# MLP up projections as seven block products of eight, on sums of token halves that stay on chip

## The chip, the cores and the metric

One Trainium2 chip, and one of its cores. A core has five engines that each run their own list of instructions strictly in order: TensorE (PE) for matmuls, VectorE (DVE), ScalarE (ACT), GpSimd (POOL) and SyncE (SP); they wait for one another by semaphores, and DMA queues move data between HBM and the core's memory, SBUF. Matmul results land in eight banks of PSUM. The metric is the time of one execution on the device, in microseconds; the figure for a kernel is the median of several executions.

## The reference

A trunk of four layers on 512 tokens of width 1024. A layer has a token mixer (gated linear attention, latent attention, a gated convolution, gated linear attention again), then an MLP with 4096 hidden columns, then a gated per-layer embedding. The change touches the MLP alone:

```python
for i in range(DEPTH):                       # DEPTH = 4
    h = ...                                  # the mixer of layer i
    x = layer_norm(ALPHA * x + h, ln_g[i, 0], ln_b[i, 0])
    x = layer_norm(ALPHA * x + sq_relu_mlp(x, mlp_w1[i], mlp_w2[i]), ln_g[i, 1], ln_b[i, 1])
    ...                                      # the per-layer embedding

def sq_relu_mlp(x, w1, w2):                  # x 512x1024, w1 1024x4096, w2 4096x1024
    return jnp.square(jax.nn.relu(x @ w1)) @ w2
```

All of it is float32.

## The kernel before

**Three matmuls for one.** TensorE takes a reduced float32 (fp32r). To keep float32 accuracy each operand is split into a high part (a cast on ScalarE) and a low part (the operand less its high part, on VectorE); `split` (L86) does it in pieces of 128 x 1024, and `mm3` (L112) issues high by high, high by low and low by high (L114 to L116). Weights come from HBM by SyncE (`wget`, L90, four buffers of 1 MB named raw) and are split into four slots (`wsplit`, L95, tiles wh and wl). Token-side operands and hidden values are tiles r of a ring of ten buffers of 1 MB; t tiles are temporaries, xn the residual rows, ps the PSUM banks.

**The MLP** (L230). The hidden columns are taken in eight groups of 512. `up(g)` computes a group: four blocks of 128 columns, for each 8 steps of the inner dimension by three matmuls that hold 128 x 128 of the weights still and move 512 tokens (a record with `ps<-r,wh`, 128x512). Relu and square on ScalarE (L233, L234) leave the hidden tile. The first group runs in two halves of 256 tokens (128x256), because the transposes of the last tokens come in between (`ln_tr`, L160, which transposes normalised rows on TensorE and splits them). The operand x is split once, in four ring buffers.

`down(g)` (L258) takes two groups of hidden values, 512 tokens by 1024 hidden, against 1024 x 1024 of the second weights, as seven block products of eight (a block scheme of the Strassen kind). Blocks of a are formed in place on VectorE (L303, L305, L313, L315). Sums of weight blocks are made by accumulating DMAs, which GpSimd issues (`wadd`, L106): the buffer `chain` gets b22, then b12 is added, it is split for product 2, then b11 is added, split for product 3, then b21 is added, split for product 5; `both` is b12 plus b11, for product 6. Each product is 2 x 4 x 3 matmuls that move 512 weight columns (`ps<-wh,r`, 128x512). VectorE adds each result into xn (L286, L288); the last down of a layer also starts its layer norm.

**Order.** TensorE's order is the order in which the program is written: up 0, up 1, then (up 2, down 0, up 3), (up 4, down 1, up 5), (up 6, down 2, up 7), down 3. The lists of the other engines are ordered by a scheduler when the program is built. A tile from a pool waits until the instruction that last used its buffer is done, and a DMA into it waits likewise.

## Time and profile before

| | |
|---|---|
| median of three runs | 2403.24 us (2403.14 to 2404.35) |
| profiled execution's own time | 2404.62 us |
| its span | 2402.0 us |
| the four MLPs in it | 244 to 573, 808 to 1137, 1378 to 1707, 2006.5 to 2335.5 us |
| TensorE busy in the first of these | 328.86 of 329.00 us |
| HBM read, written | 323.64 MB, 8.39 MB |
| accumulating loads of 1 MB | 64 in the program, 16 a layer |
| plain loads of MLP weights of 1 MB | 144, 5.0 us to landing in the median |

The times come from the runs, the rest from one profiled execution, whose span runs from its first instruction to its last; the 2.6 us between span and own time lie around it. A view that lists instructions gives the start, the duration, the engine, the line in the program, the operation, out<-in by the program's names, and in brackets the idle time before it and what released it. A group's row gives the count, then busy time and mean duration in ns, then the engine's idle time before those instructions. Matmuls overlap: a record's duration is longer than the distance to the next one. For DMAs, "to landing" is the time from the issue until the data is there.

### The profile page before, as it was taken

The page shows a single profiled execution, that of the slowest core. Times are in us where ns is not written, and L with a number is a line of the kernel's source. Part 1 is how long each engine was busy: PE and PEld are TensorE (multiplying, and loading weights), DVE is VectorE, ACT ScalarE, POOL GpSimd, SP SyncE. Part 2 cuts the span into 40 slices and gives each one's busy share as a digit, 9 for nine tenths or more (in the row PEclk, how much of TensorE's full clock was granted, in tenths as well). Part 3 has the DMA queues.
Part 4 walks back from the last instruction along what each step waited for, and adds up shares of the span by engine and source line. Part 5 has one row for each costly group of instructions (what it writes and reads, how often), then busy time and mean ns, then how long its engine had stood idle before and what let it go on. Part 6 is the DMA issues. An engine that isn't in the chain of part 4 may idle for free. (4 is left out here: it accounts for less than half of the span.)

```text
span 2402.0 us, 28355 instructions
## 1 busy us (share of the span) xinstructions
PE 2374.6 (99%) x11394; PEld 1994.7 (83%) x11394; DVE 1549.8 (65%) x1964; ACT 1078.2 (45%) x1542; POOL 260.4 (11%) x264
## 2 busy tenths in 40 slices
PE   8999999999999999999999999999999999999998
PEld 7888888888888888888888888888887888888887
DVE  6777466469687654577744646656957766645775
ACT  6353445445464354444422244445444443544452
POOL 1541000000000100000000000000005511000000
PEclk9999999999999999999999999999999999999999
DMA  6222565674323356665424256567441224566650
GB/s 226 79 92 102 134 180 141 159 197 158 118 84 110 120 129 173 193 177 165 145 101 158 71 140 186 152 154 201 155 130 62 89 104 123 141 158 192 187 155 35
DMA packets 64563, 334.90 MB, mean 139 GB/s; under 512 B 6704, under 2 KB 19760, under 8 KB 28080
## 3 DMA queue, kind: packets, MB, share of 16 engines
q1 hardware_dynamic: 52272, 256.55, 30.6%
q0 software_dynamic: 9856, 68.16, 15.1%
q10 hardware_dynamic: 2304, 8.39, 1.0%
q8 instruction: 89, 1.46, 0.2%
q14 instruction: 42, 0.34, 0.0%
HBM read 323.64 MB, written 8.39 MB: 138 GB/s over the span
## 5 line engine op out<-in xcount | busy, mean ns | idle before, releaser
L88 DVE TENSOR_TENSOR wl<-raw,wh 128x1024 fp32r<-128x1024 f32 x510 | 623.5, 1238 | 452.2 <-ACT wh L87 448.6
L87 ACT CAST wh<-raw 128x1024 fp32r<-128x1024 f32 x510 | 520.3, 1049 | 585.0 <-PE ps L115 245.6
L114 PE MATMUL ps<-r,wh 128*128 128x512 f32 (+1 forms) x1896 | 714.9, 377 | 4.0 <-ACT r L87 4.0
L115 PE MATMUL ps<-r,wh 128*128 128x512 f32 (+1 forms) x1896 | 710.6, 375 | 1.5 <-DVE r L88 0.9
L116 PE MATMUL ps<-r,wl 128*128 128x512 f32 (+1 forms) x1896 | 710.0, 374 | 0.0
L114 PE MATMUL ps<-wh,r 128*128 128x512 f32 x1328 | 520.1, 392 | 0.0
L116 PE MATMUL ps<-wh,r 128*128 128x512 f32 x1328 | 517.0, 389 | 0.0
L115 PE MATMUL ps<-wl,r 128*128 128x512 f32 x1328 | 516.7, 389 | 0.0
L114 PEld LDWEIGHTS ps<-r,wh 128*128 128x128 f32 x1896 | 357.8, 189 | 67.3 <-ACT r L87 5.0
L115 PEld LDWEIGHTS ps<-r,wh 128*128 128x128 f32 x1896 | 357.7, 189 | 66.3 <-DVE r L88 4.2
L116 PEld LDWEIGHTS ps<-r,wl 128*128 128x128 f32 x1896 | 357.5, 189 | 63.9
L116 PEld LDWEIGHTS ps<-wh,r 128*128 128x128 f32 x1328 | 249.3, 188 | 52.2
L115 PEld LDWEIGHTS ps<-wl,r 128*128 128x128 f32 x1328 | 249.5, 188 | 50.6
L114 PEld LDWEIGHTS ps<-wh,r 128*128 128x128 f32 x1328 | 249.4, 188 | 50.5
L88 DVE TENSOR_TENSOR r<-r,r 128x1024 fp32r<-128x1024 f32 x112 | 136.4, 1221 | 80.9 <-ACT r L87 80.9
L87 ACT CAST r<-r 128x1024 fp32r<-128x1024 f32 x112 | 116.7, 1049 | 136.8 <-PE ps L116 80.2
L107 POOL DMA_DIRECT2D raw<-in_mlp_w x64 | 55.9, 874 | 1085.4 <-DVE wl L88 633.3
L288 DVE TENSOR_TENSOR xn<-xn,ps 128x512 f32<-128x512 f32 x192 | 130.6, 680 | 57.7 <-PE ps L116 57.7
L233 ACT ACTIVATE t<-ps 128x512 f32<-128x512 f32 x128 | 76.0, 594 | 143.6 <-PE ps L116 143.6
L146 POOL TENSOR_TENSOR rs<-rs,nhalf 128x1 f32<-128x1 f32 (+2 forms) x44 | 59.7, 1358 | 685.2 <-DVE rs L145 685.2
L87 ACT CAST r<-ps 128x512 fp32r<-128x512 f32 x84 | 46.5, 591 | 95.2 <-PE ps L164 80.9
L480 ACT ACTIVATE t<-t 128x512 f32<-128x512 f32 (+2 forms) x64 | 37.4, 590 | 107.0 <-POOL t L544 77.0
(192 smaller groups left out, 1864.0 us busy)
## 6 DMA issues: line engine op xcount, KB each, us to landing
raw<-in_mlp_w SPq DMA_DIRECT2D x144, 1024.0 KB, 5.0
raw<-in_mlp_w POOLq DMA_DIRECT2D x64, 1024.0 KB, 8.4
raw<-in_ple_gate SPq DMA_DIRECT2D x16, 1024.0 KB, 5.1
raw<-in_conv_in SPq DMA_DIRECT2D x12, 1024.0 KB, 5.1
raw<-in_gla_v SPq DMA_DIRECT2D x8, 1024.0 KB, 5.5
raw<-in_gla_r SPq DMA_DIRECT2D x8, 1024.0 KB, 4.9
raw<-in_gla_out SPq DMA_DIRECT2D x8, 1024.0 KB, 5.0
xd<-t SPq DMA_DIRECT2D x24, 256.0 KB, 3.9
```

The costliest lines, as they stand in the source:

```text
L87: A.copy(h, src)
L88: return V.tensor_tensor(out=l, in0=src, in1=f(h), op=ALU.subtract)
L107: G.dma_start(dst, ap, accum_op=ALU.add)
L114: PE.matmul(o, ah, bh, start=start, stop=False, skip_group_check=more)
L115: PE.matmul(o, ah, bl, start=False, stop=False, skip_group_check=more)
L116: PE.matmul(o, al, bh, start=False, stop=stop, skip_group_check=more)
L146: G.tensor_tensor(out=dst, in0=dst, in1=nhalf[:, :n], op=ALU.pow)
L233: A.activation(r, ps, AF.Relu)
L288: V.tensor_tensor(out=z, in0=z, in1=ps, op=op)
L480: exps.append(A.activation(o, a, AF.Exp, scale=1.0 / TAU))
```

## The change

**Up becomes seven products of eight.** A group of 512 hidden columns is seen as two halves of 256 columns, the inner dimension as two halves of 512, the tokens as two halves of 256. Seven products, named 1, 2, 7, 6, 4, 5, 3 in the order in which they run, take the place of eight: each multiplies a 512 x 256 block (or sum of blocks) of the weights with a 512 x 256 block (or sum) of the tokens, 2 x 4 x 3 = 24 matmuls that move 256 tokens. TensorE's list grows from 10,476 to 12,396 matmul and transpose rows.

**Token sums.** `add_norm` leaves the transposed tokens unsplit (`raw_tr`). `form(p)` makes the operand of product p in place from the quarters of x (a11, a21, a12, a22) and splits it; each is made once a layer and kept for all eight groups, in seven of now eleven ring buffers. The temporaries lose one buffer.

**Weight sums.** The host lays the first weights out in quarters. Per group: w0 (two loads of 0.5 MB, products 1 and 2), w2 (a load of 1 MB and an accumulating load of 1 MB, products 7 and 5), w3 (two VectorE adds in w0's buffer, products 6 and 4), w1 (0.5 MB, product 3).

**Results.** Products 1, 6 and 7 are copied out of PSUM by ScalarE; products 2, 4 and 5 are combined with these copies on VectorE; then relu and square as before, in the new lines L306 and L307.

**Order.** Two groups, then down, four times. The last product of a group is held and runs after products 1 and 2 of the next group, or after the first product of down; the last product of down runs after products 1 and 2 of the next group. The first two groups of a layer are interleaved (`first_groups`).

The diff, without blank lines and a few repeats:

```diff
@@ -53,9 +53,9 @@
-    r8 = ctx.enter_context(tc.tile_pool(name="r8", bufs=10))
+    r8 = ctx.enter_context(tc.tile_pool(name="r8", bufs=11))
...
-    t2 = ctx.enter_context(tc.tile_pool(name="t2", bufs=8))
+    t2 = ctx.enter_context(tc.tile_pool(name="t2", bufs=7))
...
@@ -165,6 +165,13 @@
             sl = slice(t * P, t * P + P)
             split(xh[c][:, :, sl], xl[c][:, :, sl], ps)
 
+    def raw_tr(t, z, xr):
+        for c in range(2):
+            ps = bank().rearrange("p (k q) -> p k q", q=P)
+            for k in range(4):
+                PE.transpose(ps[:, k, :], z[:, (c * 4 + k) * P : (c * 4 + k + 1) * P], ident)
+            A.copy(xr[c][:, :, t * P : t * P + P], ps)
+
     def new_xT():
         xh = [ring([P, 4, T], F32R) for _ in range(2)]
         xl = [ring([P, 4, T], F32R) for _ in range(2)]
@@ -211,8 +218,8 @@
             for t in range(NT):
                 hk = pre(t) if hf == 0 and pre else {}
                 if hf == 1 and t >= 2:
-                    new = new or [new_xT()]
-                    hk = {4: lambda t=t: ln_tr(t - 2, xn[t - 2], *new[0])}
+                    new = new or [[ring([P, 4, T]) for _ in range(2)]]
+                    hk = {4: lambda t=t: raw_tr(t - 2, xn[t - 2], new[0])}
                 ps = nat_group(lhs, ws, t, hk)
                 z = xn[t][:, hf * 512 : hf * 512 + 512]
                 if scaled:
@@ -235,28 +242,143 @@
         hid = {}
+        forms = {}
+        xq = [x[c][:, :, h * 256 : h * 256 + 256] for c in range(2) for h in range(2)]
+        def form(p):
+            if p not in forms:
+                a11, a21, a12, a22 = xq
+                if p == 7:
+                    V.tensor_tensor(out=a11, in0=a11, in1=a21, op=ALU.subtract)
+                elif p == 6:
+                    V.scalar_tensor_tensor(out=a11, in0=a11, scalar=-1.0, in1=a22, op0=ALU.mult, op1=ALU.subtract)
+                elif p == 5:
+                    V.tensor_tensor(out=a21, in0=a22, in1=a21, op=ALU.subtract)
+                elif p == 3:
+                    V.scalar_tensor_tensor(out=a11, in0=a11, scalar=-1.0, in1=a12, op0=ALU.mult, op1=ALU.subtract)
+                st = forms[p] = ring([P, 2, 4, 256], F32R)
+                split(st[:, 0], st[:, 1], {1: a11, 7: a11, 6: a11, 3: a11, 2: a12, 4: a22, 5: a21}[p])
+            return forms[p]
         def up(g):
-            ws = [v3(wload(I["mlp_w1"][i, 2 * g + u]), 256) for u in range(2)]
-            hid[g] = ring([P, 4, T])
-            if g > 0:
-                for fb in range(4):
-                    hidden_out(stat_group(ws[fb // 2], fb % 2, x), hid[g], fb)
-                return
...
+            raw = [None] * 4
+            w = {}
+            bk = {}
+            kept = {}
+            half = slice(0, 1024), slice(1024, 2048)
+            def weights(p):
+                src = I["mlp_w1"][i, g]
+                if p in (1, 2) and raw[0] is None:
+                    raw[0] = wraw.tile([P, 2048], F32, tag="raw", name=nm("raw"))
+                    for h, c in zip(half, (0, 3)):
+                        SP.dma_start(raw[0][:, h], src[:, c * 1024 : c * 1024 + 1024])
+                    w[0] = v3(wsplit(raw[0]), 256)
+                if p in (7, 5) and raw[2] is None:
+                    raw[2] = wget(src[:, 1024:3072])
+                    wadd(raw[2], src[:, 0:2048])
+                    w[2] = v3(wsplit(raw[2]), 256)
+                if p in (6, 4) and raw[3] is None:
+                    a, b = (raw[0][:, h] for h in half)
+                    V.tensor_tensor(out=a, in0=a, in1=raw[2][:, half[1]], op=ALU.add)
+                    V.tensor_tensor(out=b, in0=b, in1=a, op=ALU.add)
+                    raw[3] = raw[0]
+                    w[3] = v3(wsplit(raw[3]), 256)
+                if p == 3:
+                    raw[1] = wget(src[:, 2048:3072], 1024)
+                    w[1] = v3(wsplit(raw[1], 1024), 256)
+                n, k0 = {1: (0, 0), 2: (0, 4), 7: (2, 4), 5: (2, 0), 6: (3, 0), 4: (3, 4), 3: (1, 0)}[p]
+                return w[n], k0
+            def quarter(th, hf):
+                if g not in hid:
+                    hid[g] = ring([P, 4, T])
+                return hid[g][:, 2 * hf : 2 * hf + 2, th * 256 : th * 256 + 256]
...
+            def act(o, src, scale=1.0):
+                r = tmp()
+                A.activation(three(r), src, AF.Relu, scale=scale)
+                A.activation(o, three(r), AF.Square)
+            def product(p):
+                name = {1: "b", 2: "d", 7: "c", 6: "b", 4: "c", 5: "b", 3: "b"}[p]
+                (wh, wl), k0 = weights(p)
+                st = form(p)
+                first = name not in bk
+                if first:
+                    bk[name] = bank()
+                ps = bk[name]
+                for cb in range(2):
+                    o = ps[:, cb * 256 : cb * 256 + 256]
+                    c = slice(cb * P, cb * P + P)
+                    for k in range(4):
+                        mm3(o, (wh[:, k0 + k, c], wl[:, k0 + k, c]), (st[:, 0, k, :], st[:, 1, k, :]),
+                            first and k == 0 and cb == 0, k == 3, not first or cb == 1)
+                if p in (1, 6):
+                    t = kept[p] = tmp()
+                    A.copy(t, ps)
+                elif p == 7:
+                    t = kept[p] = tmp()
+                    A.mul(t, ps, -1.0)
+                elif p == 2:
+                    z = quarter(0, 0)
+                    V.tensor_tensor(out=z, in0=three(kept.pop(1)), in1=three(ps), op=ALU.add)
+                    act(z, z)
+                elif p == 4:
+                    z = quarter(1, 0)
+                    V.tensor_tensor(out=z, in0=three(kept.pop(6)), in1=three(ps), op=ALU.add)
+                    act(z, z)
+                elif p == 5:
+                    z = quarter(1, 1)
+                    V.tensor_tensor(out=z, in0=three(kept.pop(7)), in1=three(ps), op=ALU.subtract)
+                    act(z, z)
+                else:
+                    act(quarter(0, 1), three(ps), -1.0)
+            return product
+        held = []
+        def release():
+            while held:
+                held.pop(0)()
+        def group(g):
+            u = up(g)
+            u(1)
+            u(2)
+            release()
+            for p in (7, 6, 4, 5):
+                u(p)
+            held.append(lambda: u(3))
+        def first_groups():
+            u, n = up(0), up(1)
+            u(1)
+            raw_tr(2, xn[2], x)
+            u(2)
+            n(1)
+            raw_tr(3, xn[3], x)
+            n(2)
+            for p in (7, 6, 4, 5):
+                u(p)
+            n(7)
+            u(3)
+            for p in (6, 4, 5):
+                n(p)
+            held.append(lambda: n(3))
         def down(g, gb=None):
-            h0, h1 = hid.pop(2 * g), hid.pop(2 * g + 1)
+            h0, h1 = hid[2 * g], hid[2 * g + 1]
             lo, hi = slice(0, 256), slice(256, 512)
             a11, a21, a12, a22 = h0[:, :, lo], h0[:, :, hi], h1[:, :, lo], h1[:, :, hi]
             sts = [small(12, f"st{t}", 1) for t in range(NT)] if gb is not None else None
@@ -267,10 +389,13 @@
                 return I["mlp_w2"][i, hf, 2 * g + c]
-            def product(a, w, name, th, hf, op):
+            def ready(a, w):
                 st = ring([P, 2, 4, 256], F32R)
                 split(st[:, 0], st[:, 1], a)
-                wh, wl = v3(wsplit(w), 512)
+                return st, v3(wsplit(w), 512)
+            def product(st, w, name, th, hf, op):
+                wh, wl = w
                 for q in range(2):
                     first = (name, q) not in banks
                     if first:
@@ -299,29 +424,32 @@
             b11, b12, b21, b22 = weights(0, 0), weights(1, 0), weights(0, 1), weights(1, 1)
             chain = wget(b22)
             wadd(chain, b12)
-            product(a11, wget(b11), "b", 0, 0, add)
+            product(*ready(a11, wget(b11)), "b", 0, 0, add)
+            release()
             V.tensor_tensor(out=a11, in0=a11, in1=a21, op=sub)
-            product(a11, chain, "c", 1, 1, sub)
+            product(*ready(a11, chain), "c", 1, 1, sub)
             V.scalar_tensor_tensor(out=a11, in0=a11, scalar=-1.0, in1=a22, op0=ALU.mult, op1=sub)
             wadd(chain, b11)
-            product(a11, chain, "b", 1, 0, add)
+            product(*ready(a11, chain), "b", 1, 0, add)
             wadd(chain, b21)
-            product(a12, wget(b21), "d", 0, 0, add)
+            product(*ready(a12, wget(b21)), "d", 0, 0, add)
             both = wget(b12)
             wadd(both, b11)
-            product(a22, chain, "c", 1, 0, add)
+            product(*ready(a22, chain), "c", 1, 0, add)
             V.tensor_tensor(out=a21, in0=a22, in1=a21, op=sub)
-            product(a21, both, "b", 1, 1, sub)
+            product(*ready(a21, both), "b", 1, 1, sub)
             V.scalar_tensor_tensor(out=a11, in0=a11, scalar=-1.0, in1=a12, op0=ALU.mult, op1=sub)
-            product(a11, wget(b22), "b", 0, 1, sub)
-        up(0)
-        up(1)
-        for g in range(3):
-            up(2 * g + 2)
-            down(g)
-            up(2 * g + 3)
-        down(3, load_gb(i, 1))
+            parts = ready(a11, wget(b22))
+            held.append(lambda: product(*parts, "b", 0, 1, sub))
+            if gb is not None:
+                release()
+        first_groups()
+        for g in range(4):
+            if g:
+                group(2 * g)
+                group(2 * g + 1)
+            down(g, load_gb(i, 1) if g == 3 else None)
         return new_xT()
     def ple(i, x, xn, last):
...
+def _quad(w):
+    u = _stat(w).reshape(-1, 2, P, 2, 1024)
+    return np.concatenate([u[:, c, :, r] for r, c in ((0, 0), (0, 1), (1, 1), (1, 0))], axis=-1)
...
-    o["mlp_w1"] = np.stack([_stat(w) for w in a["mlp_w1"]])
+    o["mlp_w1"] = np.stack([_quad(w) for w in a["mlp_w1"]])
...
-    nc = bacc.Bacc("TRN2", target_bir_lowering=False, num_devices=1, dynamic_dma_scratch_size=4096)
+    nc = bacc.Bacc("TRN2", target_bir_lowering=False, num_devices=1, dynamic_dma_scratch_size=2048)
```

**How the order moves: down's fifth product.** ScalarE's list in the second down of a layer, before; raw_459 is the buffer `chain`, wh_472 its split for product 3 and wh_482 that for product 5, r_481 the operand of product 5, raw_480 the buffer `both`.

```order
L87 CAST wh_472_3125<-raw_459_3040 128x1024 [waits DMASW6_49]
L234 ACTIVATE r_450_2927<-t_454_2981 128x512 [waits Activation_49]
L87 CAST wh_472_3125<-raw_459_3040 128x1024
...
L87 CAST r_475_3160<-r_435_2798 128x1024 [waits PE_49]
L87 CAST wh_482_3203<-raw_459_3040 128x1024 [waits DMASW7_49]
L87 CAST wh_482_3203<-raw_459_3040 128x1024
L87 CAST r_481_3200<-r_435_2798 128x1024 [waits PE_49]
L87 CAST wh_485_3239<-raw_480_3197 128x1024 [waits DMASW5_49]
```

The same list in the change; raw_473 is `chain`, wh_485 its split for product 2, wh_490 for product 3, wh_500 for product 5; r_499 is the operand of product 5, raw_498 is `both` and wh_503 its split for product 6.

```order
L87 CAST wh_485_3260<-raw_473_3181 128x1024 [waits DMASW0_49,PE_49]
...
L87 CAST wh_490_3299<-raw_473_3181 128x1024 [waits DMASW2_49]
...
L87 CAST wh_500_3377<-raw_473_3181 128x1024 [waits DMASW3_49]
L87 CAST wh_500_3377<-raw_473_3181 128x1024
L87 CAST wh_503_3413<-raw_498_3371 128x1024 [waits DMASW1_49]
L87 CAST wh_503_3413<-raw_498_3371 128x1024
L87 CAST r_499_3374<-r_457_3017 128x1024 [waits DVE_49,PE_49]
```

The operand of product 5 now stands behind the split of the sixth product's weights, not ahead of it. The wait for PE at wh_485 is for the slot that product 4 of the second group used last; the semaphore DMASW is that of the accumulating load.

**How the order moves: the first groups.** ScalarE's list in the change, from the last transposes on (r_334 and r_335 are the raw tokens, r_371 the operand of product 7, r_376 that of product 6; wh_388 is the split of a 0.5 MB weight for product 3, in a slot that products 1 and 2 of the second group used last):

```order
L173 COPY r_335_1903<-ps_364_2122 128x4x128 [waits PE_49]
L87 CAST wh_388_2337<-raw_387_2335 128x1024 [waits DMAHW0_49,PE_49]
L87 CAST r_371_2168<-r_334_1902 128x1024 [waits DVE_49]
L306 ACTIVATE t_367_2155<-r_366_2153 128x512 [waits DVE_49]
L307 ACTIVATE r_366_2153<-t_367_2155 128x2x256 [waits Activation_49]
L87 CAST r_376_2207<-r_334_1902 128x1024 [waits DVE_49]
```

And VectorE's at the same place:

```order
L255 TENSOR_TENSOR r_334_1902<-r_334_1902 128x4x256 [waits Activation_49]
...
L88 TENSOR_TENSOR wl_389_2338<-raw_387_2335,wh_388_2337 128x1024 [waits DMAHW0_49,Activation_49]
L88 TENSOR_TENSOR r_371_2168<-r_334_1902,r_371_2168 128x1024 [waits Activation_49]
L257 SCALAR_TENSOR_TENSOR r_334_1902<-r_334_1902,r_335_1903 128x4x256 [waits DVE_49]
L88 TENSOR_TENSOR r_376_2207<-r_334_1902,r_376_2207 128x1024 [waits Activation_49]
```

Before, the tokens' splits stood here, straight out of the transposes; now a weight's cast and its subtraction come ahead of the operand of product 7, and three operations in place stand between the transposes and the operands.

11 lines of the change are left out of this document (2 added, 9 removed).

## The prediction

> **What bounds the kernel now.** I read the busy times first, then the slices, then the groups, then stretches.
>
> ```profile
> span 2402.0 us, 28355 instructions
> PE 2374.6 (99%) x11394; PEld 1994.7 (83%) x11394; DVE 1549.8 (65%) x1964; ACT 1078.2 (45%) x1542; POOL 260.4 (11%) x264
> PE   8999999999999999999999999999999999999998
> DVE  6777466469687654577744646656957766645775
> DMA  6222565674323356665424256567441224566650
> ```
>
> TensorE is busy 99% of the span and no other engine comes near. The stretch of the first MLP (from 244 to 573 us; the other three are alike) shows the same:
>
> ```profile
> core 0: us, PE busy (x) PEld busy (x) DVE busy (x) ACT busy (x) POOL busy (x), PEclk, DMA share, GB/s
> 244.00:573.00 329.00, 328.86 (x1550) 276.42 (x1549) 200.59 (x207) 152.06 (x183) 17.04 (x18) 1.00 0.61 168
> ```
>
> TensorE pauses 0.14 us in 329. So each matmul taken away is paid in full, and each new wait of TensorE costs in full. VectorE, at 200.59 of 329 (61%), and the DMA engines, at 0.61, have room, but not endless room.
>
> **The gain: matmuls times spacing.** A matmul record's duration overlaps the next one, so I take the spacing from starts that lie far apart in unbroken runs:
>
> ```profile
> 394.28 0.39 PE L114 MATMUL ps<-wh,r 128*128 128x512 f32 x1
> ...
> 424.20 0.39 PE L114 MATMUL ps<-wh,r 128*128 128x512 f32 x1
> 245.45 0.28 PE L114 MATMUL ps<-r,wh 128*128 128x256 f32 x1
> ...
> 247.61 0.28 PE L114 MATMUL ps<-r,wh 128*128 128x256 f32 x1
> ```
>
> The 512-wide pair is 132 matmuls apart: 29.92 / 132 = 0.2267 us. The 256-wide pair is 18 apart: 2.16 / 18 = 0.120 us. Two halves therefore cost 0.240, 6% more than one whole.
>
> Per layer, up has been seven groups of 4 x 8 x 3 = 96 wide matmuls (672) and the first group in halves (192 narrow): 672 x 0.2267 + 192 x 0.120 = 175.4 us. It becomes 8 groups x 7 products x 24 = 1344 narrow ones: 161.3 us. The gain is 14.1 us a layer, 56.4 in all; of the 23.1 that seven wide products would save (672 x 0.2267 = 152.3), 9.0 go to the narrow form. Down keeps its 7 x 24 wide matmuls per call, 5.44 us a product.
>
> [...]
>
> **What is added beside TensorE.** The rows that price it:
>
> ```profile
> L88 DVE TENSOR_TENSOR wl<-raw,wh 128x1024 fp32r<-128x1024 f32 x510 | 623.5, 1238 | 452.2 <-ACT wh L87 448.6
> L87 ACT CAST wh<-raw 128x1024 fp32r<-128x1024 f32 x510 | 520.3, 1049 | 585.0 <-PE ps L115 245.6
> L88 DVE TENSOR_TENSOR r<-r,r 128x1024 fp32r<-128x1024 f32 x112 | 136.4, 1221 | 80.9 <-ACT r L87 80.9
> L305 DVE SCALAR_TENSOR_TENSOR r<-r,r 128x1024 f32<-128x1024 f32 x16 | 19.6, 1223 | 0.4
> L233 ACT ACTIVATE t<-ps 128x512 f32<-128x512 f32 x128 | 76.0, 594 | 143.6 <-PE ps L116 143.6
> L288 DVE TENSOR_TENSOR xn<-xn,ps 128x512 f32<-128x512 f32 x192 | 130.6, 680 | 57.7 <-PE ps L116 57.7
> ```
>
> A group has seven split pieces on VectorE instead of four, two adds of raw weights and three additions out of PSUM; 3 x 1.24 + 2 x 1.22 + 3 x 0.68 = 8.2 us a group, 65 a layer, and 13 more for the seven token sums with their splits, less the eight splits of 512 columns that the old transposes had. VectorE goes to about 275 of 330, 83%. ScalarE gets 24 more casts, 24 PSUM copies and seven casts of sums: 24 x 1.05 + 24 x 0.59 + 7 x 1.05 = 47 more, 60%. A group loads 3.5 MB instead of 2 (0.5 + 0.5, 1 plus an accumulated 1, 0.5), 12 MB more a layer on the 168 GB/s x 329 us = 55 MB there now: the DMA share goes from 0.61 to about 0.75. All three stay under TensorE, so averages cost nothing; I walked the steady cycle (two groups and a down, 14 x 2.88 + 7 x 5.44 = 78.4 us of TensorE) engine by engine, and looked for places where something comes late in order. The PSUM copies, the smaller ring of temporaries, the eleventh ring buffer and the smaller scratch I cost at nothing: their consumers lie several products behind. If that cover is gone, a late PSUM copy is one row of 0.59 us per product, at most 56 x 0.59 = 33 us a layer if all were bare, which I leave out of the range, since ScalarE has 40% of its time free.
>
> **First wait: the first groups.** The tokens' transposes now come raw, and the sums are made after them. Product 1 waits for the VectorE split of its sum behind the layer norm's tail, about 0.8 us beyond its place. Product 7 needs the sum a11 - a21. On ScalarE its cast stands behind a weight cast (wh_388) whose slot is freed only when the second group's product 2 ends, and that is the last work ahead of product 7. VectorE's order has that weight's split ahead of the sum's as well. So from there 1.05 (weight cast) + 1.24 (its split, with the sum's cast beside it) + 1.22 (the sum's split) = 3.5 us. Product 6 needs an update (1.22), a cast (0.95 back to back) and a split (1.22), 3.6 with hand-overs against product 7's 24 x 0.120 = 2.9: 0.7. Together 5.0, less the 0.3 that the start of an MLP waits today (two starts 0.42 apart below, where 0.12 is the spacing), 4.7 a layer. Bounds for product 7: with the slot free early, the sum's own cast and split, 2.3; with the sum's subtraction late too, 1.22 more, 4.7. So 3.5 to 5.9 a layer.
>
> ```profile
> 243.99 0.28 PE L114 MATMUL ps<-r,wh 128*128 128x256 f32 x1
> 244.41 0.39 PE L115 MATMUL ps<-r,wh 128*128 128x256 f32 x1
> ```
>
> **Second wait: the fifth product of down.** Its weights are b22 + b12 + b11 + b21, one buffer to which two accumulating loads are added after its earlier contents are split. The rows of today:
>
> ```profile
> L107 POOL DMA_DIRECT2D raw<-in_mlp_w x64: 857/866/1049, 252.2 to 2297.8; - x64
> DMA to landing us min/median/max: 7.8/8.4/14.8
> L107 POOL DMA_DIRECT2D raw<-in_mlp_w x8: 864/867/876, 343.6 to 470.7; - x8
> DMA to landing us min/median/max: 7.9/8.2/11.7
> 456.60 1.23 DVE L88 TENSOR_TENSOR wl<-raw,wh 128x1024 fp32r<-128x1024 f32 x1 [0.20 <-ACT wh L87]
> 458.13 0.87 POOL L107 DMA_DIRECT2D raw<-in_mlp_w  x1 [13.76 <-DVE wl L88]
> 466.18 1.05 ACT L87 CAST wh<-raw 128x1024 fp32r<-128x1024 f32 x1
> 470.70 0.88 POOL L107 DMA_DIRECT2D raw<-in_mlp_w  x1 [11.70 <-DVE wl L88]
> 481.51 1.06 ACT L87 CAST r<-r 128x1024 fp32r<-128x1024 f32 x1 [2.66 <-PE ps L116]
> 482.48 1.99 ACT L87 CAST wh<-raw 128x1024 fp32r<-128x1024 f32 x2
> ```
>
> A split's end at 457.83 gives an issue at 458.13 (0.3 us), and 466.18 is the cast that waits for its landing (8.05). The second load, issued at 470.70, lands by some 478.9, and its cast starts at 482.48, behind another cast: 3.6 us of slack, because the chain was begun early, under an up group.
>
> In the change the slot for the chain's first split comes free when the second group's product 4 ends (t = 0; a group's products run in the order 1, 2, 7, 6, 4, 5, 3), since the buffers hold that group's weights until then. From there, all with the rows above: cast 1.15, a relu and square between, second cast 2.65, split 3.9, issue 4.2, landing 4.2 + L; cast, cast and split 3.5, issue 0.3, landing L again; then ScalarE's order has five casts (0.95 each back to back, as two in 1.99 show): two of the chain, two of the weights for the sixth product, and only then the operand's own, r_499; VectorE splits it by 7.0 after the landing. With the shortest L, 7.9: 12.1, 16.0, 23.9, 30.9. TensorE meanwhile: product 5 of the group to 2.88, first down product to 8.32, the held product 3 to 11.20, then 16.64, 22.08, 27.52; the fifth product's third matmul is due at 27.97. It waits 3.0 us. Each further microsecond of L counts twice. This happens in the first three cycles of a layer; in the fourth the operand's cast stands ahead, which gives 4.7 us back (1.7 to spare).
>
> L is the choice that decides. The rows give 7.9 at the least, 8.2 to 8.4 as the median, 11.7 at the most in this stretch. The change puts more transfers beside these two (another accumulation and three to five plain loads run meanwhile), so I take 8.8, a little above the median: 4.8 us in three cycles and 0.1 in the fourth, 14.5 a layer. Down's remaining products are fed by casts that are done by then; who waits behind r_499 on ScalarE (the casts for products 6 and 7) has 5.44 us of TensorE work ahead.
>
> **The sum.** Per layer -14.1 + 4.7 + 14.5 = +5.1; four layers +20.4. On the span 2402.0 + 20.4 = 2422.4; on that execution's own time, 2404.62, it is 2425.0. The median of the runs, 2403.24, lies 1.4 below that execution, so I forecast **2424 us**. With L from 8.4 to 9.4 the waits are 12.0 to 19.3 a layer, and the time 2414 to 2443; with a third to half a microsecond a layer on either side for the first groups, its own range is 2412 to 2445.
>
> **Rivals.** (1) *The fifth product doesn't wait.* If the weights' slot or the casts come earlier than the order tells, or the load is shorter than any of the 64, only the first groups' cost is left: 4 x (4.7 - 14.1) = -37.6, **2366 us**. For it: TensorE waits for nothing in the MLPs today, with the same chain. Against: slots and casts are fixed by in-order queues, and even at the shortest landing the operand is done 3.0 us after 27.97; from there on it decides. [...]
>
> (2) *Landings at their shortest.* With L = 7.9 all along, the waits are 9.0 a layer: 4 x (-14.1 + 4.7 + 9.0) = -1.6, **2402 us**, no change. For it: the queue of accumulating loads is not asked for two at a time in the chain. Against: half the landings are above 8.4 already.
>
> (3) *The transfers get in each other's way.* With L = 11.7, as the longest here, the waits are 10.6 in three cycles and 5.9 in the fourth, 37.7 a layer: 4 x 28.3 = +113, **2516 us**; half-way, L = 10.2, it is 2467. It takes over from L of about 9.5. For it: 12 MB more a layer, and a maximum of 14.8 in the table. Against: the share stays at about 0.75.
>
> **How the numbers follow.** Forecast 0.52, rival (1) 0.14, (2) 0.18, (3) 0.16. The likeliest is 2424. A measurement of this kernel tells 0.2%, 4.8 us, from no change. Faster: (1) and a third of (2), whose own spread is 2392 to 2411: 0.20. Same: the middle of (2), with the forecast's lower edge: 0.12. Slower: 0.68. The range is 2372 to 2465: it leaves out the lower half of (1), 0.07, and most of (3), 0.11.
>
> **What would show it.** Right: 4 x 1344 narrow matmuls where 4 x 192 were; TensorE's idle before it put on ScalarE's r casts and VectorE's r splits; in each of the first three cycles of an MLP a pause of 3 to 6 us in down, with the accumulation's landing about 8.8; a pause near 3.5 in the first groups. Wrong: no pause in down (then 1), pauses under a weight cast rather than r, landings over 10 (3), a narrow spacing that isn't 0.120, or VectorE without gaps, which would mean that its 83% is the bound after all.

## The result, and the profile after

The changed kernel takes **2513.14 us** (median of four runs, 2508.31 to 2515.88) against 2403.80 for the kernel before (four runs as well): a ratio of 1.0451, 95% interval 1.0433 to 1.0470. The forecast was 2424, with a range up to 2465: right in sign, far too small. The profiled execution took 2513.02 us, its span is 2510.9, so 108.9 more than the span before.

The page of the changed kernel, its first lines:

```profile
span 2510.9 us, 33039 instructions
PE 2382.9 (95%) x13314; PEld 2072.8 (83%) x13314; DVE 1810.7 (72%) x2232; ACT 1242.9 (49%) x1762; POOL 294.7 (12%) x296
```

TensorE is busy 95% instead of 99%, and its busy time did not fall by 56 us; it rose by 8. (The profile counts 13,314 matmul and transpose records where it counted 11,394; the lists counted under the change are 918 shorter on either side, so the growth of 1,920 is the same.) The first MLP, by stretch (the columns are those of the stretch shown before):

```profile
245.00:595.00 350.00, 325.95 (x2013) 291.76 (x2011) 254.83 (x259) 192.28 (x238) 20.59 (x23) 0.97 0.69 185
```

329 us have become about 350, and the granted clock of TensorE is 0.97 there, where it was 1.00. VectorE is at 73% and the DMA share at 0.69, both below what the prediction allowed for. Who TensorE waits for, over the whole span (total us, times, longest):

```profile
PE ps L114 <- ACT r L87: 45.3, 22, 5.5
PE ps L116 <- DVE r L88: 16.6, 20, 1.3
PE ps L114 <- DVE xn L413: 15.2, 4, 4.2
PE ps L114 <- DVE r L339: 12.2, 9, 3.1
PE ps L115 <- DVE r L88: 8.3, 13, 1.1
```

Before, two of these rows are there, and they are small:

```profile
PE ps L114 <- ACT r L87: 8.8, 5, 4.8
PE ps L115 <- DVE r L88: 0.9, 4, 0.2
```

ScalarE's r casts and VectorE's r splits are the operands that the prediction named. Two are new kinds: L339, VectorE's sum for product 5 of a group, which TensorE needs before it may add product 3 into the same bank; and L413, VectorE's reading of a bank in down.

**Half speed.** The pauses cost more than their own length here: 44.7 us of half speed over the span, by the ledger below. Down's fifth product in the second cycle, TensorE's list:

```profile
402.87 0.39 PE L116 MATMUL ps<-wh,r 128*128 128x512 f32 x1
405.80 0.50 PE L114 MATMUL ps<-wh,r 128*128 128x512 f32 x1 [2.55 <-ACT r L87]
406.13 0.40 PE L115 MATMUL ps<-wl,r 128*128 128x512 f32 x1
407.87 0.80 PE L116 MATMUL ps<-wh,r 128*128 128x512 f32 x1 [1.34 <-DVE r L88]
408.46 0.63 PE L114 MATMUL ps<-wh,r 128*128 128x512 f32 x1
408.89 0.63 PE L115 MATMUL ps<-wl,r 128*128 128x512 f32 x1
...
413.15 0.63 PE L116 MATMUL ps<-wh,r 128*128 128x512 f32 x1
413.58 0.47 PE L114 MATMUL ps<-wh,r 128*128 128x512 f32 x1
413.89 0.40 PE L115 MATMUL ps<-wl,r 128*128 128x512 f32 x1
```

And two stretches there:

```profile
408.00:413.50 5.50, 5.50 (x13) 4.38 (x14) 5.50 (x7) 3.74 (x4) 0.87 (x1) 0.50 0.71 229
413.50:420.00 6.50, 6.50 (x29) 5.32 (x28) 4.66 (x6) 0.00 (x0) 0.00 (x0) 0.98 0.99 222
```

After the two pauses twelve matmuls start 0.43 us apart instead of 0.2267, with a granted clock of 0.50 by the stretch; then it is 0.98 again.

**A ledger.** From the starts of consecutive matmuls in the trace I took the excess over 0.2267 or 0.120 us; an excess of 65% to 115% of the spacing is put down as half speed, any other above 0.03 as pause. The table gives us over the span, by place: "first groups" is the first 30 us of an MLP, "downs 1 to 3" and "last downs" are the four downs of a layer, "outside" is what lies outside the MLPs; the names e1 to e8 are those of the experiments below.

| kernel | first groups | downs 1 to 3 | groups | last downs | outside | half speed |
|---|---|---|---|---|---|---|
| changed | 18.6 | 56.5 | 19.4 | 28.5 | 24.3 | 44.7 |
| e1, products exchanged | 17.4 | 35.1 | 11.1 | 20.7 | 23.7 | 20.7 |
| e4, operand first | 18.1 | 6.4 | 94.7 | 25.7 | 25.2 | 46.1 |
| e5, w2 first | 18.4 | 52.0 | under 0.1 | 20.8 | 23.0 | 31.7 |
| e6, both | 18.0 | 8.5 | 9.8 | 21.0 | 22.2 | 21.1 |
| e7, exchanged and w2 first | 18.4 | 38.3 | under 0.1 | 12.2 | 23.9 | 19.2 |
| e8, e7 with pins | 15.3 | 8.8 | under 0.1 | 11.8 | 21.6 | 9.4 |

The kernel before has 23.2 us of pauses and 6.0 of half speed in all, of which 1.2 of pauses are at the start of its MLPs. The span of the changed kernel from this: 2402.0 - 56.4 + (147.3 - 23.2) + (44.7 - 6.0) = 2508.4, against 2510.9 measured. The same sum for the six others comes out 2 to 3 us below their spans.

### The profile page after: what moved, and what is told of

It is laid out like the page before. It is cut to its first block, busy times and chain, and to the rows that moved or that the text cites. A ratio compares the mean times of both kernels' runs of the same rounds, so it can differ in the third digit from the quotient of the medians.

```text
span 2510.9 us, 33039 instructions
## 1 busy us (share of the span) xinstructions
PE 2382.9 (95%) x13314; PEld 2072.8 (83%) x13314; DVE 1810.7 (72%) x2232; ACT 1242.9 (49%) x1762; POOL 294.7 (12%) x296
## 5 line engine op out<-in xcount | busy, mean ns | idle before, releaser
L88 DVE TENSOR_TENSOR wl<-raw,wh 128x1024 fp32r<-128x1024 f32 x606 | 733.7, 1229 | 316.5 <-ACT wh L87 310.0
L87 ACT CAST wh<-raw 128x1024 fp32r<-128x1024 f32 x606 | 613.2, 1046 | 641.2 <-DMA raw<-in_mlp_w 341.1
L114 PE MATMUL ps<-r,wh 128*128 128x256 f32 (+1 forms) x2536 | 808.2, 319 | 28.1 <-DVE r L339 12.2
L115 PE MATMUL ps<-r,wh 128*128 128x256 f32 (+1 forms) x2536 | 802.0, 316 | 8.3 <-DVE r L88 8.3
L116 PE MATMUL ps<-r,wl 128*128 128x256 f32 (+1 forms) x2536 | 800.5, 316 | 0.0
L114 PE MATMUL ps<-wh,r 128*128 128x512 f32 x1328 | 535.4, 403 | 45.3 <-ACT r L87 27.9
L116 PE MATMUL ps<-wh,r 128*128 128x512 f32 x1328 | 532.3, 401 | 16.7 <-DVE r L88 16.6
L114 PEld LDWEIGHTS ps<-r,wh 128*128 128x128 f32 x2536 | 488.2, 193 | 64.2 <-DVE r L339 14.0
L115 PEld LDWEIGHTS ps<-r,wh 128*128 128x128 f32 x2536 | 488.5, 193 | 41.3 <-DVE r L88 12.0
L116 PEld LDWEIGHTS ps<-r,wl 128*128 128x128 f32 x2536 | 488.1, 192 | 29.1
L88 DVE TENSOR_TENSOR r<-r,r 128x1024 fp32r<-128x1024 f32 x140 | 170.0, 1221 | 37.9 <-ACT r L87 37.7
L87 ACT CAST r<-r 128x1024 fp32r<-128x1024 f32 x140 | 144.1, 1048 | 88.5 <-DVE r L429 32.9
L413 DVE TENSOR_TENSOR xn<-xn,ps 128x512 f32<-128x512 f32 x192 | 129.3, 677 | 0.0
L286 DVE TENSOR_TENSOR raw<-raw,raw 128x1024 f32<-128x1024 f32 x32 | 38.7, 1221 | 77.5 <-DMA raw<-in_mlp_w 77.5
L306 ACT ACTIVATE t<-r 128x512 f32<-128x512 f32 x96 | 60.6, 631 | 63.8 <-DVE r L335 37.6
```

Source lines behind the costliest of these rows:

```text
L87: A.copy(h, src)
L88: return V.tensor_tensor(out=l, in0=src, in1=f(h), op=ALU.subtract)
L114: PE.matmul(o, ah, bh, start=start, stop=False, skip_group_check=more)
L115: PE.matmul(o, ah, bl, start=False, stop=False, skip_group_check=more)
L116: PE.matmul(o, al, bh, start=False, stop=stop, skip_group_check=more)
L286: V.tensor_tensor(out=a, in0=a, in1=raw[2][:, half[1]], op=ALU.add)
```

## The experiments

There were two theories at first. **A**: the prediction's, a late operand and late weights at the fifth product, with half speed after each pause. **B**: the transfers are in each other's way, and a wait that is removed only moves on. The first four runs led to a third, **C**.

### e1: fifth and sixth product exchanged

```diff
-            product(*ready(a22, chain), "c", 1, 0, add)
             V.tensor_tensor(out=a21, in0=a22, in1=a21, op=sub)
             product(*ready(a21, both), "b", 1, 1, sub)
+            product(*ready(a22, chain), "c", 1, 0, add)
```

> The changed kernel with down's fifth and sixth products exchanged, in all downs: the product of both comes before that of chain. Theory A (TensorE waits for the operand and weights of the fifth product, and after such a pause of 3 to 5 us it runs some 6 to 12 matmuls at twice their spacing): in the trace of the changed kernel these twelve places cost about 51 us of pauses and 93 matmuls x 0.2 = 19 us of half speed. The exchange gives the chain 5.4 us more; what is left is a cast of the new fifth product's operand that stands behind the chain's casts, about 1.5 us a place without half speed: 51 + 19 - 18 = 52 us less. The last down's 4.2 us wait for VectorE's read of a bank goes as well, since another product now lies between the two that share the bank: 4 x 4.2 + half speed 4 x 1.5 = 23 less. Together about 2438. Theory B (transfers are the limit; the wait only moves to the next product that needs a landing): less than 20 us gained, 2495 to 2513, with new pauses at the sixth product.

Measured: 2448.24 us, 1.0183 of before (1.0164 to 1.0203). 65 less, near A's 75, far from B. In the ledger downs lose 21, groups 8, last downs 8, half speed 24. Groups weren't expected to lose anything.

### e2: one accumulation left out

```diff
-            wadd(chain, b21)
```

> The changed kernel without the accumulation of b21 into chain, so the fifth product of each down uses a wrong block sum; everything else is as before. Theory A: the fifth product no longer waits for the second landing, the 51 us of pauses and 19 us of half speed go, and nothing else changes: about 2443 (2435 to 2455). Theory B (accumulating loads in each other's way): with 16 of 96 gone the others land sooner, so the waits at the start of the next group go as well, another 19 us and more: below 2425. If it is neither, the pause stays for the operand's cast, which would then be what decides: above 2480.

Measured: 2414.42 us, 1.0038 of before (1.0023 to 1.0053). 99 less, more than all the pauses of downs 1 to 3 with their half speed (56.5 + 19). The time lies where B put it, but not for B's reason: the landing of the accumulations that are left did not get shorter, median 9.7 us against 9.3. What got shorter is the cycle: from the accumulation of b11 in one down to that in the next it is 78.8 to 81.5 us, and 83.1 to 88.6 in the changed kernel. So one link of 9 us out of a chain shortened everything behind it, without making other transfers faster. Neither theory says that.

### e3: the order alone

The kernel before, with group, group, down:

```diff
-        up(0)
-        up(1)
-        for g in range(3):
-            up(2 * g + 2)
-            down(g)
-            up(2 * g + 3)
-        down(3, load_gb(i, 1))
+        for g in range(4):
+            up(2 * g)
+            up(2 * g + 1)
+            down(g, load_gb(i, 1) if g == 3 else None)
```

> The kernel before with full up products, but in the changed kernel's order: group, group, down, four times a layer. Theory A: with two weight slots a group the chain's first slot is free half a group earlier, and ScalarE and VectorE have room; no wait at the fifth product, within 6 us of the kernel before: 2398 to 2410. Rival: the order itself leaves the chain too late, since no group runs between the loads of a down and its products: twelve pauses of 3 to 4 us with half speed after them, 2440 to 2480.

Measured: 2405.04 us, ratio 1.0000 (0.9991 to 1.0009). The order of groups and downs costs nothing by itself; the accumulations land after 8.0 us in the median there. So it is what the change adds to that order that matters.

### e4: the operand's cast ahead

```diff
+                if first:
+                    cast = A.copy(st[:, 0], a)
+                    V.tensor_tensor(out=st[:, 1], in0=a, in1=f(st[:, 0]), op=ALU.subtract)
+                    with tc.issue_after(cast.ins):
+                        return st, v3(wsplit(w), 512)
                 split(st[:, 0], st[:, 1], a)
                 return st, v3(wsplit(w), 512)
...
-            product(*ready(a22, chain), "c", 1, 0, add)
+            product(*ready(a22, chain, True), "c", 1, 0, add)
```

> The changed kernel with one thing moved: the cast of the fifth product's operand is pinned ahead of the chain's weight casts on ScalarE. Theory A: the operand is ready 5 us earlier, the end of the chain is then the split of its weights; with landings of 9 us about 1.5 us of pause are left at each of twelve places and the half speed after them goes: 51 + 19 - 18 = 52 less, about 2461. If the landing and not the operand's place decides: less than 15 us gained, 2498 or more.

Measured: 2538.06 us, 1.0559 of before (1.0542 to 1.0577): 25 **more** than the changed kernel. A's 52 less is missed by 77 us; the time lies within the second expectation (2498 or more), which did not expect a loss, nor where it stands. Whom TensorE waits for, e4:

```profile
PE ps L114 <- DVE r L339: 79.4, 12, 7.2
PE ps L114 <- ACT r L87: 17.4, 9, 5.5
```

The fifth product's wait is gone as A had it (downs 6.4 instead of 56.5), and a wait of up to 7.2 us stands in the groups behind each of these twelve downs instead (94.7 in groups instead of 19.4). Whatever sets the length of a cycle is neither the operand's place nor the group's sum.

### Theory C: a loop through one buffer

GpSimd's accumulating loads in the changed kernel, one cycle (the third accumulation of `chain`, issued at 392.51, then w2 of the first group, w2 of the second, the next chain's b12, `both`, and the next chain's b11 and b21), and SyncE's load of w2 for the first group, last row:

```profile
392.51 0.87 POOL L107 DMA_DIRECT2D raw<-in_mlp_w  x1 [12.33 <-DVE wl L88]
410.69 0.87 POOL L107 DMA_DIRECT2D raw<-in_mlp_w  x1 [17.31 <-DVE r L88]
433.89 0.87 POOL L107 DMA_DIRECT2D raw<-in_mlp_w  x1 [22.34 <-DVE wl L88]
437.81 0.87 POOL L107 DMA_DIRECT2D raw<-in_mlp_w  x1 [3.05 <-DMA raw<-in_mlp_w]
462.19 0.88 POOL L107 DMA_DIRECT2D raw<-in_mlp_w  x1 [23.51 <-DVE r L429]
467.87 0.87 POOL L107 DMA_DIRECT2D raw<-in_mlp_w  x1 [4.81 <-DVE wl L88]
481.01 0.87 POOL L107 DMA_DIRECT2D raw<-in_mlp_w  x1 [12.27 <-DVE wl L88]
404.98 0.33 SPq L92 DMA_DIRECT2D raw<-in_mlp_w  x1
```

In the built program the four raw buffers are handed on so that the one that `chain` leaves goes to w2 of the first group, and the one that this leaves to w2 of the second. The issue times fit: the load at 404.98 follows the end of `chain`'s last split, and the load for the second group follows the add that reads the first group's w2 last:

```profile
426.92 1.22 DVE L286 TENSOR_TENSOR raw<-raw,raw 128x1024 f32<-128x1024 f32 x1
428.21 0.33 SPq L92 DMA_DIRECT2D raw<-in_mlp_w  x1
```

So the links follow each other: chain's third accumulation and its split (392.51 to 404.98: 12.5 us), the load of w2 (5.7), its accumulation, split and add, then the second group's load (23.2 to 433.89), the second group's accumulation, its sums and products and the new chain's first split (34.0 to 467.87), the second accumulation (13.1 to 481.01). That is 88.5 us for a cycle in which TensorE has 78.4 us of work. A layer has three such cycles; from b11 to b11 the twelve take 83.1 to 88.6 us, 1037 in all. How the late w2 reaches TensorE, in the second layer, VectorE and then TensorE:

```profile
948.81 1.23 DVE L286 TENSOR_TENSOR raw<-raw,raw 128x1024 f32<-128x1024 f32 x1 [7.33 <-DMA raw<-in_mlp_w]
954.67 0.68 DVE L339 TENSOR_TENSOR r<-t,ps 128x512 f32<-128x512 f32 x1
955.40 0.39 PE L114 MATMUL ps<-r,wh 128*128 128x256 f32 x1 [2.29 <-DVE r L339]
```

VectorE stands 7.33 us at the add that needs w2's landing, and the sum behind it in its list is late for TensorE. By C a wait taken away in one place comes back in another (e4), a link taken out shortens the cycle (e2), and e1 helped beyond its place because there w2 gets the buffer of `both`, which is free before chain's (from `chain`'s last accumulation to w2's it is 13.5 to 14.9 us in e1, 17.5 to 19.2 in the changed kernel).

### e5: w2 loaded ahead of w0

```diff
+                if raw[2] is None:
+                    raw[2] = wget(src[:, 1024:3072])
+                    wadd(raw[2], src[:, 0:2048])
                 if p in (1, 2) and raw[0] is None:
```

> The changed kernel with the loads of w2 issued ahead of those of w0 in every group, so that w2 gets the buffer of down's fourth product's weights and w0 the one that chain leaves. Theory C (a loop through one buffer: chain's third landing and split, then the load and accumulation of w2 of the first group in the same buffer, its split, then those of w2 of the second group again in it, then TensorE's products, whose end starts the next chain; it takes 86 to 90 us a cycle where TensorE has 78.4 us of work): the loop is cut, the waits at the start of the groups (19 us) go, but the fifth product's pause stays, since it hangs on the end of the second group alone, and grows from about 4.4 to the 5.2 us that the walk gives at landings of 9 us: about 2500, 2488 to 2508. Theory B (transfers in each other's way): no change, 2505 to 2520.

Measured: 2475.93 us, 1.0290 of before (1.0270 to 1.0311), 37 less than the changed kernel, and below the range that I gave C. The twelve cycles fell from 1037 to 1001 us together, which is nearly the whole gain. The groups' waits are gone (below 0.1 us of 19.4), as C says; the pauses in downs stay (52.0 of 56.5). They did not grow: the walk's 5.2 us stood on landings of 9, and `chain`'s two loads behind its first split landed after 8.4 us in the mean here, 8.6 in the changed kernel. The profiled execution is 9 us faster than the median here, so its ledger is somewhat on the low side.

### e6: w2 first and the operand first

> Both moves together: w2 ahead of w0, and the fifth product's operand cast ahead of chain's weight casts. Alone the latter took away the fifth product's pauses and gave 25 us more, with pauses of 5.7 to 7.2 us where a group's product 3 waits for VectorE, behind a wait for w2. Theory C: with the loop cut as well neither pause is left, 12 x 6.5 us and some half speed less than 2538: about 2450, 2435 to 2470. Theory B: the landings still come as late, above 2500.

Its edit is e4's and e5's together. Measured: 2422.69 us, 1.0079 of before (1.0064 to 1.0095). The move that alone cost 25 us brings 53 once the loop is cut (2475.93 to 2422.69), and both together 90; that is below the range given for C. GpSimd's list in e6, the same links:

```profile
383.47 0.86 POOL L107 DMA_DIRECT2D raw<-in_mlp_w  x1 [10.93 <-DVE wl L88]
394.55 0.86 POOL L107 DMA_DIRECT2D raw<-in_mlp_w  x1 [10.21 <-DMA raw<-in_mlp_w]
409.72 0.86 POOL L107 DMA_DIRECT2D raw<-in_mlp_w  x1 [14.31 <-DVE xn L419]
424.33 0.87 POOL L107 DMA_DIRECT2D raw<-in_mlp_w  x1 [13.75 <-DVE raw L288]
...
451.82 0.87 POOL L107 DMA_DIRECT2D raw<-in_mlp_w  x1 [5.33 <-DVE wl L88]
464.15 0.86 POOL L107 DMA_DIRECT2D raw<-in_mlp_w  x1 [11.46 <-DVE wl L88]
```

The accumulation into w2 of the second group is issued 26.3 us after chain's third accumulation, not 41.4, and this cycle takes 80.7 us (383.47 to 464.15). All 96 accumulations are still there, so B falls as the main cause. It is not empty: the accumulation into the first group's w2 landed after 9.5 to 11.7 us in the changed kernel's cycles and after 8.4 to 9.4 in e6, so one or two of a cycle's microseconds lie in slower landings.

### e7: e1 and e5 together

> The fifth and sixth products exchanged, and w2 ahead of w0. The exchange alone already gave w2 the buffer of both, which is free before chain's, and reached 2448; cycles there are 81 to 83 us. Theory C: with w2 in a buffer that is free earlier still, the group's waits of about 1 us a cycle go: 2436, 2428 to 2445. Theory B: no change, 2445 to 2452.

Measured: 2431.22 us, 1.0101 of before (1.0084 to 1.0118), 17 less than e1 and within the range given for C, with no wait left in the groups. Downs still have 38.3 us.

### e8: and two pins

```diff
-                    w[1] = v3(wsplit(raw[1], 1024), 256)
+                    with ExitStack() as pins:
+                        for ins in formed[7] if g == 0 else ():
+                            pins.enter_context(tc.issue_after(ins))
+                        w[1] = v3(wsplit(raw[1], 1024), 256)
...
-            product(*ready(a22, chain), "c", 1, 0, add)
+            product(*ready(a22, chain, tuple(last)), "c", 1, 0, add)
```

The first holds the 0.5 MB weight's split of the first group behind the cast and split of product 7's operand (`formed[7]`); the second holds chain's last split behind those of the operand made before it (`last`).

> The same with two places pinned on ScalarE and VectorE: chain's weight split behind the operand of the product of both, and in the first groups the 0.5 MB weight's split behind the operand of product 7. Theory: each in-order queue's late item is moved out of the way; the sixth place's pause of about 1.5 us goes at twelve places (18 us) and 1.2 us in the first groups at four (5 us): 22 us below the run with the exchange and w2 ahead, about 2414, 2405 to 2425. If VectorE itself is the limit by now, less than 8 us below it.

Measured: **2386.84 us**, 0.9926 of before (0.9911 to 0.9941), 44 less than e7, double what was expected: downs lose 30 instead of 18, half speed 10 that I had not counted. It is 0.7% faster than the kernel before. Its page and whom TensorE waits for (L253 and L87 are splits and casts of operands):

```profile
span 2385.9 us, 33065 instructions
PE 2330.2 (98%) x13314; PEld 2045.0 (86%) x13314; DVE 1812.7 (76%) x2232; ACT 1247.2 (52%) x1762; POOL 291.3 (12%) x296
```

```profile
PE ps L115 <- DVE r L253: 11.0, 12, 1.6
PE ps L114 <- ACT r L87: 9.7, 5, 5.7
```

Beside the changed kernel (1810.7 us of VectorE, 1242.9 of ScalarE, 96 accumulations) the engines do the same work in 125 us less. So no engine's work and no amount of transfers was the bound; the order of hand-overs was.

### e9 and e10: pauses made on purpose

The kernel before, with the low half of down's fifth operand written again by VectorE, twice (e9) or four times (e10):

```diff
                 split(st[:, 0], st[:, 1], a)
+                for _ in range(again):
+                    V.tensor_tensor(out=st[:, 1], in0=a, in1=f(st[:, 0]), op=ALU.subtract)
```

> The kernel before, with full up products; the low half of down's fifth operand is written two times more by VectorE (same values), so that TensorE must pause there, in each of 16 downs. By the order of VectorE's list and the durations of the trace of before the operand comes about 2.4 us late. Theory (a pause by itself drops TensorE to half speed for some microseconds): 16 x 2.4 = 38 us of pauses, and matmuls at 0.43 us behind them, 5 to 10 a place, 16 to 32 us more: 2458 to 2475, with a granted clock near 0.99. Rival (the half speed comes from the load on the other engines and the DMAs that the change adds): only the pauses, 2435 to 2447, and spacings of 0.23 right behind them.

> The same with four writes more: the operand comes about 8 us late. Theory: 16 x 8 = 128 us of pauses and some 10 matmuls at 0.43 us behind each, 32 us more: about 2565, granted clock 0.98. Rival: 128 us alone, about 2530, with full speed behind the pauses.

Measured: 2443.01 us for e9 (1.0159 of before, 1.0139 to 1.0180) and 2481.91 for e10 (1.0321, 1.0300 to 1.0342). By time alone e9 lies in the rival's range and e10 below both expectations, but the times can't decide here, for the doses landed elsewhere than meant: three downs of four hid e9's writes and showed only 1.6 us of e10's, and in the last down of each layer they sent VectorE's list behind a layer norm, a pause of 7.3 us. What stands behind the pauses still answers the question. e10 first, then e9, TensorE's list:

```profile
333.52 0.39 PE L115 MATMUL ps<-wl,r 128*128 128x512 f32 x1
335.37 0.50 PE L116 MATMUL ps<-wh,r 128*128 128x512 f32 x1 [1.46 <-DVE r L274]
335.71 0.40 PE L114 MATMUL ps<-wh,r 128*128 128x512 f32 x1
335.94 0.39 PE L115 MATMUL ps<-wl,r 128*128 128x512 f32 x1
```

```profile
582.61 0.79 PE L116 MATMUL ps<-wh,wl 128*128 128x512 f32 x1 [7.09 <-DVE rs L145]
...
585.34 0.63 PE L115 MATMUL ps<-wl,wh 128*128 128x512 f32 x1
585.76 0.63 PE L116 MATMUL ps<-wh,wl 128*128 128x512 f32 x1
...
588.93 0.39 PE L116 MATMUL ps<-wh,wl 128*128 128x512 f32 x1
```

A pause of 1.6 us is followed by full speed, one of 7 us by half speed for about 6 us, both in a kernel without the change's extra transfers. So in these two traces half speed came with the long pause alone, without the load that the change adds. Of the price of 16 to 32 us in e9 only 4 came, as there were 4 long pauses and not 16.

### e11: the adds behind the sum

```diff
+                    with ExitStack() as pins:
+                        for ins in joined[-1:]:
+                            pins.enter_context(tc.issue_after(ins))
+                        V.tensor_tensor(out=a, in0=a, in1=raw[2][:, half[1]], op=ALU.add)
+                        V.tensor_tensor(out=b, in0=b, in1=a, op=ALU.add)
```

`joined` holds the sums of product 5 (L339 in the changed kernel); the two adds are those that make w3.

> The changed kernel with one move on VectorE: the two adds that make w3 stay behind the sum of product 5 of the group before. In the changed kernel they stand ahead of it and wait for the accumulation into w2, and TensorE's product 3 waits for that sum (12 us in all, up to 3.1 a place). If VectorE's order is the cause, these 12 us and some half speed behind them go: 2490 to 2500. Theory C (the loop through one buffer sets the cycle, whatever the order within it): the pause moves to the product that needs w2's or w3's weights, and the time stays: 2505 to 2517.

Measured: 2533.57 us, 1.0541 of before (1.0523 to 1.0558), 20 more than the changed kernel. It lies above both ranges. That VectorE's order alone is the cause falls. In its trace the second and third cycles of the layers take 85.0 to 88.7 us from b11 to b11, 86.4 to 88.6 in the changed kernel, as C says; what is added comes in the first cycle of a layer, 91.1 to 93.6 instead of 83.1 to 85.3, where the same pin holds back the interleaved groups (the first `both` is issued at 291.7 instead of 286.0 us). C had not expected that part.

### e12: one pin more on e8

```diff
                 elif p == 5:
-                    V.tensor_tensor(out=a21, in0=a22, in1=a21, op=ALU.subtract)
+                    with tc.issue_after(formed[6][1]):
+                        V.tensor_tensor(out=a21, in0=a22, in1=a21, op=ALU.subtract)
```

> The run with the exchange, w2 ahead and the two pins, and one pin more: in the first groups the subtraction for product 5's operand, which is wanted last, stays behind the split of product 6's. In the run without it that subtraction stood 1.1 us long ahead of the split that product 7 waits for (TensorE paused 1.6 us there, and 0.5 at product 6). If VectorE's order sets that pause: 4 layers x 1.2 to 1.7 us, 5 to 7 us below 2387: 2380 to 2382. If the cast or the sum out of PSUM beside it sets it: within 2 us of 2387.

Measured: 2387.11 us, 0.9921 of before (0.9908 to 0.9935): the same as e8. Product 7's pause went only from 1.6 to 1.25 us, for the sum out of PSUM ahead of that split then waits for TensorE's own matmuls (0.89 us). The second expectation holds.

## Why the prediction was wrong

**The gain: right.** The narrow spacing is 0.120 us in the changed kernel too, and in all seven ledgers -56.4 us closes the sum to 2 or 3 us.

**First wait, the first groups: right in size.** 18.6 us measured, 4 x 5.0 = 20.0 expected; product 7 paused 2.12 + 1.33 = 3.45 us where 3.5 was worked out.

**Second wait, the fifth product: right in mechanism, somewhat over-sized.** 56.5 us in downs 1 to 3, where 14.5 x 4 = 58 was expected; that they agree so closely is in part luck, since only 49.9 of them stand at the fifth product, 2.6 to 3.0 in the first cycle of a layer and 3.9 to 5.3 in the two behind it, and the rest at other products of down. L was well chosen: the two loads of `chain` that it stands for landed after 8.6 us in the mean, where 8.8 was taken. In e5, where no group is late, the step's own formula can be tested at these loads' mean of 8.4: 12 x (3.0 + 2 x 0.5) = 48, against 47.9 measured at the fifth product. e4 shows, though, that in the changed kernel the cycle was held elsewhere as well: with this wait gone, another took its place.

**What failed, first: "I walked the steady cycle".** The walk began each cycle at the end of the group's product 4, as though the group before it were always on time. It followed chain to the fifth product and stopped there. It did not go on: whose buffer does the next load take, when is that landed, and does it come round to the start of the next cycle? That is the loop of 83 to 89 us around 78.4 us of work; by the ledger it is 19.4 us of pauses in the groups that the sum had at nothing. e5 and e6 show it.

**Second: "Down's remaining products are fed by casts that are done by then".** In the last down of a layer product 7 follows product 6 at once and adds into the same bank, so TensorE waits up to 4.2 us for VectorE's reading of it, behind splits and layer norm; weights were late there too, by up to 0.8 us at a time. 28.5 us in all. With another product between the two (e7) 12.2 are left.

**Third, and largest: a pause was priced at its own length.** 38.7 us more of half speed. The trace of before had the row that could have told it, 2.19 us of waiting and then matmuls at 0.43:

```profile
54.09 1.28 PE L555 MATMUL ps<-t,t 128*128 128x128 f32 x8 [2.19 <-POOL t L549]
...
55.60 0.63 PE L115 MATMUL ps<-r,wh 128*128 128x512 f32 x1
56.03 0.63 PE L116 MATMUL ps<-r,wl 128*128 128x512 f32 x1
```

Together: groups 19.4, last downs 28.5, half speed 38.7, elsewhere 2.3, what the ledger leaves open 2.5, less 1.4 and 1.5 by which the two waits came out shorter: the 88.5 us by which 108.9 exceeds the 20.4 forecast.

**The rivals.** Rival (3) gave 2516 us, close to the result, but for a reason that did not happen: it needed landings of 11.7 us. The view of the accumulating loads of the changed kernel:

```profile
DMA to landing us min/median/max: 7.9/9.3/13.6
```

Even with 9.3 the prediction's formula gives 2440 (3 x 5.8 + 1.1 = 18.5 a layer), `chain`'s own loads took 8.6, and e8 reaches 2387 at a median of 8.9. (The half-way case of that rival, L = 10.2, comes to 2469 by the formula, not 2467.) Rival (1) fell: TensorE did wait at the fifth product, 49.9 us in all, and none of the 96 landed under 7.9 us. VectorE as the bound, named among what would prove the prediction wrong, fell as well (72%, and 76% in the faster e8).

**Open.** e4's twelve cycles take 1061 us where the changed kernel's take 1037, and these 23 us are nearly all of its 25. The link that grew is the one from the accumulation into the second group's w2 to the next b11, 35.4 to 38.2 us instead of 32.7 to 34.9; that accumulation landed after 11.1 to 13.6 us, 8.1 to 10.9 in the changed kernel. Slower landings are what B expects, but whether other transfers slowed them, and why the moved cast would bring that about, was not tried apart. The halved scratch, the eleventh ring buffer and the smaller ring of temporaries were not tried alone; e8 keeps all three and is faster than the kernel before, so they are not what cost 109 us.

## What to carry to other kernels

Walk a steady cycle until it closes: note for each buffer who takes it next, and add the links all the way round; if the sum is longer than the busiest engine's work, that sum is the cycle, and a wait removed on the way only moves. Before costing an added chain of loads, ask which buffer its first load waits for; a change in the order of two requests for buffers was worth 37 us alone and made another move, which cost 25 by itself, worth 53. And price a pause of TensorE above its length where the trace shows half speed behind pauses of that size (here behind 38 of the 39 above 3.25 us that stood alone).

## What the runs showed of the hardware

How long the pauses were that half speed followed: over twelve traces, those of the changed kernel and of every experiment but e3, I took the pauses that stand alone (no other above 0.5 us within 8 us). Up to 1.25 us none was followed by it, but for four that lie behind a 7 us pause and those in the first microseconds of an execution; of those near 1.5 us 2 of 27 were, of those from 1.75 to 3.25 us 8 of 18, above that 38 of 39. Why some of the pauses from 1.75 to 3.25 us were and others weren't is not shown. The stretches behind lasted 2 to 6 us.
